# RWKV chunk step: the four small-matmul bursts of a chunk in one run, outputs in two alternating result banks

## The chip, the cores and the metric

The kernel runs on one core of a Trainium2 chip. The metric is device time in microseconds. The kernel before was timed in three runs: 2193.45, 2198.98 and 2200.49 us, median 2198.98. One more execution was profiled; it took 2194.43 us, of which 2192.7 us lie between the first and the last instruction (the span).

## The reference

One decoder layer over 2048 tokens of width 1024. After a norm, one wide projection feeds three branches: A, RWKV-7 time mixing with 8 heads of 64; B, sliding-window attention; C, attention over 256 memory tokens. Each branch is gated, projected back, and the three are summed by sigmoid gates, projected once more and added to x. The change is in branch A. Its heart is a recurrence over tokens, with a 64 x 64 state S for each head:

```python
def step(S, inp):
    r_t, w_t, k_t, v_t, a_t, b_t = inp
    sa = jnp.einsum('bhvk,bhk->bhv', S, a_t)
    S = S * w_t[:, :, None, :] + sa[..., None] * b_t[:, :, None, :] + v_t[..., None] * k_t[:, :, None, :]
    y = jnp.einsum('bhvk,bhk->bhv', S, r_t)
    return S, y
```

All is computed in float32. Large matmuls are done in three passes: each operand is split into a high and a low part of a shorter float32 format, and high x high, low x high and high x low are added up.

## The kernel before, in words

**Stages.** The 2048 tokens are worked in four superblocks of 512. In each, two streams of work are woven together: `stream_r` is branch A, `stream_f` is everything else that needs no result of A (memory attention, sliding-window attention, the merges of C and B, and eight gates). Then come the merge of A and the output phase (L1253 to L1268), and the next superblock. Nearly all of TensorE's instructions are dense matmuls of 128 x 128 x 512 in the helper `gemm3` (lines L471, L472, L473).

**Branch A.** `rwkv_prep` and `rwkv_inverse` turn each superblock into eight chunks of 64 tokens and park the per-chunk operands in DRAM. `rwkv_chain` (L863 on) then walks through the chunks one after another. The 8 heads lie as 4 pairs, a pair's two heads in the lower and upper 64 partitions. A chunk c needs from the chunk before it the state (in the tile Z), and does this:

- W (L928): 8 small matmuls from Q and Z into a bank of the tag `rw`. They use all 128 rows and half the columns of the array (128*64 in the profile; each matmul appears as two, so 16 in a burst).
- VectorE copies W to SBUF (L932).
- U (L943): 8 matmuls from B and W. They use a quarter of the array each (64*64).
- VectorE scales U into Z (L949, two instructions); S (L951), 4 matmuls of 128 x 128, makes the new state, and VectorE adds the decayed old one (L952, with SP from L941) into the next chunk's Z.
- The output of the chunk is a sum of two parts: `from_w` (L907), 8 matmuls from Q and Z in the form 128*64, and `from_u` (L902), 8 matmuls from B and U in the form 64*64. `from_w` comes first and starts the sum.

**Result bank.** The outputs of two chunks (`per` = 2) share one PSUM bank, `yps`. There is one such bank. When both chunks are in it, ScalarE copies it out (L912, in `take_y`), and only then may `from_w` of the next chunk start it anew. In an odd chunk the bursts come in the order W, `from_w` and then U, `from_u` of the chunk before. In an even chunk other than 0 (`later` in the code) it is W, `from_u` of the chunk before (which completes the bank), then U, and `from_w` behind it.

**What sets the order.** The engines' order is written out by a planner inside the kernel (`steps`, `lay_out`, `order`). It takes all instructions with their estimated durations and hand-over times, plays them through, and at each step gives an engine the ready instruction of lowest rank (a matmul of the array form now in use goes first). It then chains every engine's instructions in that order. A list of matmuls given to `together` becomes ready as one, and `behind` puts one instruction behind another; other matmuls may come between two such bursts.

**Pools.** PSUM has eight banks: two `mm` for dense results, two `rw`, two `as_` (attention, the transposes of the row scales and half of the output phase), one `oo` and one `yps`. `gp` is a pool of NG = 10 SBUF tiles of 2 KB per partition, named `g` in the profile, used by attention, gates, the parts of the merged result in the output phase and the rows of x loaded there (L1266) and added to the result (L1267). `dk` and `Pl` hold a superblock's per-chunk factors, two buffers each.

## Time and profile before

| | before |
|---|---|
| median of 3 runs | 2198.98 us (2193.45 to 2200.49) |
| profiled execution | 2194.43 us |
| its span | 2192.7 us |
| TensorE busy | 2168.5 us, 99% |
| VectorE, ScalarE busy | 1544.2 us, 818.7 us |
| chain bursts: L928, L907, L943, L902 | 512 matmuls each |
| bank copies L912 | 16 |

In a line of the timeline, the first number is the start in microseconds from the begin of the span, the second the length of the (merged) piece. Then come engine, line of the kernel, operation, the tile written and the tiles read, the form, and the number of instructions. A bracket at the end names idle time of the engine before it and what ended it. Matmuls overlap: the length of a dense one is longer than the distance to the next. PE is TensorE, DVE VectorE, ACT ScalarE, POOL GpSimd, SP the engine that issues most DMAs.

### The profile page before, as it was taken

How to read it: one execution, taken by the hardware profiler on the slowest of the kernel's cores; microseconds unless marked ns; L12 is line 12 of the kernel's file. 1: busy time of each engine (PE TensorE's matmuls, PEld its weight loads, DVE VectorE, ACT ScalarE, POOL GpSimd, SP SyncE). 2: the span in 40 equal slices, each digit the busy share in tenths (PEclk: the TensorE clock that was granted, in tenths of full speed). 3: DMA queues.
4: the chain of work that ended last, by engine and by line, in shares of the span. 5: the costliest groups of instructions: out<-in, count | busy, mean ns of one | idle time of the engine just before them, and what ended most of it. 6: DMA issues, size and time to landing. Idle time of an engine off the chain costs nothing.

```text
span 2192.7 us, 36285 instructions
## 1 busy us (share of the span) xinstructions
PE 2168.5 (99%) x13562; PEld 1793.1 (82%) x13562; DVE 1544.2 (70%) x3661; ACT 818.7 (37%) x1748; POOL 132.5 (6%) x166
## 2 busy tenths in 40 slices
PE   8999999999999999999999999999999999999999
PEld 7888788887888888888888888888878888887887
DVE  7789999567478889644537988954455798894332
ACT  5665554236344443203414434410423434430220
POOL 1001000001000000001000000000100010000100
PEclk9999999999999999999999999999999999999999
DMA  6978787978966566665776656675677666658456
GB/s 207 357 268 278 245 295 256 333 250 312 351 208 205 170 215 209 224 222 183 272 259 205 200 183 202 200 261 183 226 241 250 192 190 214 202 168 289 161 188 208
DMA packets 253151, 508.65 MB, mean 232 GB/s; under 512 B 38192, under 2 KB 119344, under 8 KB 252976
## 3 DMA queue, kind: packets, MB, share of 16 engines
q1 hardware_dynamic: 236848, 476.97, 65.4%
q10 hardware_dynamic: 16128, 29.37, 4.0%
q8 instruction: 107, 1.75, 0.3%
q14 instruction: 68, 0.56, 0.1%
HBM read 372.56 MB, written 133.69 MB: 231 GB/s over the span
## 4 chain that ended last, share of the span: by engine, by line
PE 90%; DMA 5%; DVE 3%; ACT 1%; issue 1%; POOL 0%; SPq 0%; ACTq 0%; DVEq 0%; POOLq 0%
PE mm L473 22%; PE mm L471 22%; PE mm L472 22%; PE oo L1212 1%; PE rw L951 1%; PE mm L1260 1%; PE mm L1261 1%; PE mm L1262 1%; PE rw L943 1%; PE rw L928 1%; PE yps L902 1%; PE yps L907 1%; PE rw L773 1%; PE rw L793 1%; DMA big<-fb 1%
## 5 line engine op out<-in xcount | busy, mean ns | idle before, releaser
L472 PE MATMUL mm<-hL,whl 128*128 128x512 f32 x1888 | 744.2, 394 | 0.0
L471 PE MATMUL mm<-hH,whl 128*128 128x512 f32 x1888 | 744.2, 394 | 0.0
L473 PE MATMUL mm<-hH,whl 128*128 128x512 f32 x1888 | 743.8, 394 | 0.0
L473 PEld LDWEIGHTS mm<-hH,whl 128*128 128x128 f32 x1888 | 354.8, 188 | 72.1 <-issue 1.2
L472 PEld LDWEIGHTS mm<-hL,whl 128*128 128x128 f32 x1888 | 354.8, 188 | 70.8 <-issue 0.7
L471 PEld LDWEIGHTS mm<-hH,whl 128*128 128x128 f32 x1888 | 354.8, 188 | 69.9 <-issue 0.3
L453 ACT ACTIVATE whl<-raw 128x512 fp32r<-128x512 f32 x178 | 111.3, 629 | 141.0 <-PE mm L473 93.8
L471 PE MATMUL mm<-yh,whl 128*128 128x512 f32 x384 | 151.3, 394 | 2.2 <-ACT gt L1228 1.5
L473 PE MATMUL mm<-yh,whl 128*128 128x512 f32 x384 | 151.7, 395 | 0.0
L472 PE MATMUL mm<-yl,whl 128*128 128x512 f32 x384 | 150.5, 392 | 0.0
L454 DVE TENSOR_TENSOR whl<-raw,whl 128x512 fp32r<-128x512 f32 x178 | 121.2, 685 | 36.9 <-ACT whl L453 35.7
L1228 ACT ACTIVATE gt<-mm 128x512 f32<-128x512 f32 x64 | 38.1, 595 | 209.0 <-PE mm L473 206.8
L830 DVE STREAM_SHUFFLE ibc<-Nc 128x496 f32<-128x496 f32 (+30 forms) x248 | 114.2, 472 | 0.1
L831 DVE TENSOR_TENSOR ibc<-ibc,Yi 128x496 f32<-128x496 f32 (+30 forms) x248 | 104.4, 421 | 3.7
L832 DVE TENSOR_TENSOR Yi<-Yi,ibc 128x496 f32<-128x496 f32 (+30 forms) x248 | 102.8, 414 | 0.7
L1267 DVE SCALAR_TENSOR_TENSOR g<-mm,g 128x512 f32<-128x512 f32 x16 | 11.1, 692 | 112.1 <-PE mm L1262 87.8
L471 PEld LDWEIGHTS mm<-yh,whl 128*128 128x128 f32 x384 | 72.1, 188 | 18.2 <-ACT gt L1228 1.7
L473 PEld LDWEIGHTS mm<-yh,whl 128*128 128x128 f32 x384 | 72.1, 188 | 14.7
L472 PEld LDWEIGHTS mm<-yl,whl 128*128 128x128 f32 x384 | 72.1, 188 | 14.6
L1243 DVE SCALAR_TENSOR_TENSOR gt<-gt,mm 128x512 f32<-128x512 f32 x32 | 22.0, 687 | 75.9 <-PE mm L473 75.6
L1185 ACT ACTIVATE g<-g,mxs,st 128x128 f32<-128x128 f32 x128 | 61.5, 484 | 25.9 <-DVE mxs L1178 25.9
L436 POOL TENSOR_SCALAR st<-st 128x4 f32<-128x4 f32 (+1 forms) x32 | 11.4, 355 | 938.9 <-DVE st L1027 434.6
(1801 smaller groups left out, 3600.4 us busy)
## 6 DMA issues: line engine op xcount, KB each, us to landing
whl<-k SPq DMA_DIRECT2D x486, 512.0 KB, 3.7
k<-whl SPq DMA_DIRECT2D x162, 512.0 KB, 4.8
raw<-in_w_in SPq DMA_DIRECT2D x118, 256.0 KB, 3.7
fq<-big SPq DMA_DIRECT2D x64, 256.0 KB, 4.6
fb<-big SPq DMA_DIRECT2D x64, 256.0 KB, 4.7
big<-fq SPq DMA_DIRECT2D x32, 512.0 KB, 6.2
big<-fb SPq DMA_DIRECT2D x32, 512.0 KB, 5.8
g<-in_x ACTq DMA_DIRECT2D x32, 256.0 KB, 5.2
```

The source lines that it names most:

```text
L453: S.activation(w[:, 0], raw, AF.Copy)
L454: V.tensor_tensor(w[:, 1], raw, w[:, 0].bitcast(F32), op=ALU.subtract)
L471: PE.matmul(out, lh, rh, start=i == 0, stop=False)
L472: PE.matmul(out, lh, rl, start=False, stop=False)
L473: PE.matmul(out, ll, rh, start=False, stop=i == n - 1)
L773: m = PE.matmul(g[:, c], BK[h, c0 + c], Q[h, c0 + c], start=True, stop=True)
L830: V.stream_shuffle(bc[:, :, :w], N_[:, :, s + 1:], [s] * 32)
L831: V.tensor_tensor(bc[:, :, :w], bc[:, :, :w], Y[:, :, s:s + 1].to_broadcast([128, n, w]), op=ALU.mult)
L832: V.tensor_tensor(Y[:, :, s + 1:], Y[:, :, s + 1:], bc[:, :, :w], op=ALU.add)
L1185: S.activation(P_, P_, AF.Exp, scale=r2[:, b, i:i + 1], bias=mx[:, b, i:i + 1], accum_out=mx[:, b, 2 + i:3 + i])
L1228: S.activation(t, gp, AF.Tanh, scale=0.5)
L1243: V.scalar_tensor_tensor(g, g, 1.0, pp, op0=ALU.add, op1=ALU.mult)
```

## The change

Within `rwkv_chain`, W, `from_w` of the same chunk and `from_u` of the chunk before become one burst, in that order, for every chunk. U is tied to the last matmul of that burst: a new table `follow` tells the planner that after this matmul TensorE takes nothing but U, and waits for it if need be. In chunk 0 there is no `from_u`, and no tie. Since `from_w` of a new pair now comes ahead of the `from_u` that completes the pair before, two result banks are in use by turns: `yps`, and one of the two `as_` banks. The pool of `g` tiles grows from 10 to 11, and `dk` and `Pl` go from two buffers to one.

```diff
-NG = 10
+NG = 11
...
-def steps(instructions, manual, groups, ahead=1000):
+def steps(instructions, manual, groups, follow, ahead=1000):
...
+    for a, b in follow.items():
+        byname[a].next = byname[b]
...
-    tile, wires, table = (128, 128), 0, 2
+    tile, wires, table, held = (128, 128), 0, 2, None
...
         for e, rs in ready.items():
+            if e == "PE" and held:
+                rs = {held: rs[held]} if held in rs else {}
             if rs:
...
-        can = [s for s, t in ready[e].items() if t <= at]
+        can = [s for s, t in ready[e].items() if t <= at and (e != "PE" or held in (None, s))]
...
-            tile = s.tile
+            tile, held = s.tile, s.next
...
+        ys = {}
+
         def yslot(i, c, e):
-            return yps[OD if (c + e) % 2 else EV, i, c % per // 2, e]
+            return ys[c // per][OD if (c + e) % 2 else EV, i, c % per // 2, e]
...
-            S.activation(full, yps.rearrange("p i t e v -> p (i t e v)"), AF.Copy)
+            S.activation(full, ys[last // per].rearrange("p i t e v -> p (i t e v)"), AF.Copy)
...
-            later = c % per == 0 and c
+            if c % per == 0:
+                ys[c // per] = (s_ps if c // per % 2 else y_ps)().rearrange("p (i t e v) -> p i t e v", i=n, t=per // 2, e=2)
             pw = rw_ps()[:, :n * C].rearrange("p (i t) -> p i t", i=n)
-            prev = burst([PE.matmul(pw[h, i], Q[:, i, e, :C], Z[:, i, e], start=True, stop=True) for i, e, h in HH], None, upds)
-            if later:
-                burst(from_u(c - 1), prev)
+            prev = burst([PE.matmul(pw[h, i], Q[:, i, e, :C], Z[:, i, e], start=True, stop=True) for i, e, h in HH] + from_w(c) + (from_u(c - 1) if c else []), None, upds)
             W = rp.tile([128, n, C], F32, name="W", bufs=1)
             V.tensor_copy(W, pw)
-            if later:
+            if c and c % per == 0:
                 take_y(c - 1)
-            if c % per == 0:
-                yps = y_ps().rearrange("p (i t e v) -> p i t e v", i=n, t=per // 2, e=2)
-            if not later:
-                burst(from_w(c), prev)
...
-            prev = burst([PE.matmul(pu[h, i], B[h, i, 0, :C], W[h, i], start=True, stop=True) for i, e, h in HH])
-            if later:
-                prev = burst(from_w(c), prev)
-            elif c:
-                prev = burst(from_u(c - 1), prev)
+            us = [PE.matmul(pu[h, i], B[h, i, 0, :C], W[h, i], start=True, stop=True) for i, e, h in HH]
+            if c:
+                follow[prev.ins.name] = us[0].ins.name
+            prev = burst(us, prev)
...
-            dk = xp.tile([128, 4, NC_], F32, name="dk", bufs=2)
-            Pl = xp.tile([128, 4, NC_], F32, name="Pl", bufs=2)
+            dk = xp.tile([128, 4, NC_], F32, name="dk", bufs=1)
+            Pl = xp.tile([128, 4, NC_], F32, name="Pl", bufs=1)
```

## The prediction

> **What bounds the kernel now.** I read the page first: busy time, clock, chain of waits.

> ```profile
> span 2192.7 us, 36285 instructions
> PE 2168.5 (99%) x13562; PEld 1793.1 (82%) x13562; DVE 1544.2 (70%) x3661; ACT 818.7 (37%) x1748; POOL 132.5 (6%) x166
> PE 90%; DMA 5%; DVE 3%; ACT 1%; issue 1%; POOL 0%; SPq 0%; ACTq 0%; DVEq 0%; POOLq 0%
> ```

> TensorE is idle for 2192.7 − 2168.5 = 24.2 us, and 90% of the chain that ended last lies on it. What sets the time is therefore how many nanoseconds pass from the start of one matmul to the start of the next. Busy time hides that, since overlapping matmuls count once; only the start column of the timeline shows it. Here is TensorE's timeline through two neighbouring chunks of the chain, c = 1 and c = 2 (start, length, line, tile, rows*columns of the array, count).

> ```profile
> 409.07 0.39 PE L473 MATMUL mm<-hH,whl 128*128 128x512 f32 x1
> 409.39 0.69 PE L928 MATMUL rw<-Zt,big 128*64 128x64 f32 x16
> 409.91 0.64 PE L907 MATMUL yps<-Zt,big 128*64 128x64 f32 x16
> 410.47 0.50 PE L471 MATMUL mm<-hH,whl 128*128 128x512 f32 x1
> 410.90 0.68 PE L943 MATMUL rw<-W,big 64*64 64x64 f32 x16
> 411.42 0.63 PE L902 MATMUL yps<-Zt,big 64*64 64x64 f32 x16
> 411.98 0.50 PE L472 MATMUL mm<-hL,whl 128*128 128x512 f32 x1
> 412.32 0.39 PE L473 MATMUL mm<-hH,whl 128*128 128x512 f32 x1
> ...
> 415.05 0.39 PE L472 MATMUL mm<-yl,whl 128*128 128x512 f32 x1
> 415.37 0.69 PE L928 MATMUL rw<-Zt,big 128*64 128x64 f32 x16
> 415.99 0.68 PE L902 MATMUL yps<-Zt,big 64*64 64x64 f32 x16
> 416.60 0.50 PE L473 MATMUL mm<-yh,whl 128*128 128x512 f32 x1
> 417.03 0.68 PE L943 MATMUL rw<-W,big 64*64 64x64 f32 x16
> 417.64 0.69 PE L907 MATMUL yps<-Zt,big 128*64 128x64 f32 x16
> 418.26 0.50 PE L471 MATMUL mm<-yh,whl 128*128 128x512 f32 x1
> 418.59 0.39 PE L472 MATMUL mm<-yl,whl 128*128 128x512 f32 x1
> 418.82 0.40 PE L473 MATMUL mm<-yh,whl 128*128 128x512 f32 x1
> ```

> L928 is W, L943 is U, L907 the output part from Z and Q (call it Yq), L902 the output part from U (Yu). Dense matmuls, L471 to L473, follow each other every 0.23 us (418.59 to 418.82). The step from a dense one into a burst takes 0.32 (409.07 to 409.39), the first dense one after a burst holds TensorE for 0.34 (411.98 to 412.32), and a single dense one between two bursts for 0.43 (410.47 to 410.90). A burst of 16 takes 0.52 when a burst of its own form follows (409.39 to 409.91), 0.56 to 0.62 when another form follows (409.91 to 410.47, 415.37 to 415.99).

> **The burst order, the main term.** The steady chunks have one dense matmul between the two visits (one of the 28 has two). Odd chunk: W, Yq | dense | U, Yu. Even chunk, where a result bank is finished and the next begun: W, Yu | dense | U, Yq. After the change both are W, Yq, Yu, U: two 128*64 bursts, then two 64*64 ones. No matmul is added or removed.

> Odd chunk. Before, from 409.07 to 412.32: 3.25 us with three dense matmuls in it. After: 0.32 + 0.52 + 0.56 + 0.52 + 0.56 + 0.34 = 2.82 with two of them; the displaced one runs elsewhere for 0.23, so 3.05. Saved: 0.20, which is 0.43 − 0.23: it is the lone dense matmul that is dear.

> Even chunk. Before, from 415.05 to 418.59: 3.54. After: the same 3.05. Saved: 0.49, since W, Yu and U, Yq each also changed form inside the visit.

> Chunks of these two kinds: c = 1, 3, 5, 7 and c = 2, 4, 6 in each of four superblocks, 16 and 12. Chunk 0 keeps its two visits, as it has no earlier Yu and its U is not tied; the last Yu runs alone as before. The last of the 28, an odd one, has W to U in the 1.51 us of the first (409.39 to 410.90):

> ```profile
> 2056.35 0.69 PE L928 MATMUL rw<-Zt,big 128*64 128x64 f32 x16
> ...
> 2057.86 0.68 PE L943 MATMUL rw<-W,big 64*64 64x64 f32 x16
> ```

> Sum: 16 × 0.20 + 12 × 0.49 = 9.1 us off TensorE. As dense work is waiting at every one of these places, I count all of it as time off the end. No DMA is added, and a chunk's fetch stands where it stood; its buffers come free with Yu, which in odd chunks is now ahead of U, so no later.

> **The wait that the lone dense matmul covered.** U reads W from SBUF, so VectorE must have copied it (L932). Nothing may run on TensorE between Yu and U now, so whatever the copy is late becomes idle TensorE, with all queued dense matmuls behind it. VectorE's copy, and what came before and after it, in three chunks:

> ```profile
> 410.12 0.42 DVE L932 COPY W<-rw 128x256 f32<-128x256 f32 x1 [0.46 <-PE rw L928]
> ...
> 954.55 0.43 DVE L949 TENSOR_TENSOR Zt<-rw,dk 64x256 f32<-64x256 f32 x1
> 955.03 0.71 PE L951 MATMUL rw<-Zt,big 128*128 128x128 f32 x4
> ...
> 471.26 0.69 PE L928 MATMUL rw<-Zt,big 128*64 128x64 f32 x16
> 471.58 0.69 DVE L454 TENSOR_TENSOR whl<-raw,whl 128x512 fp32r<-128x512 f32 x1 [1.14 <-ACT whl L453]
> ...
> 472.30 0.42 DVE L932 COPY W<-rw 128x256 f32<-128x256 f32 x1
> ```

> W starts at 409.39 and the copy ends at 410.54, 1.15 us later. The hand-over from VectorE to TensorE is not shown for an idle array and this pair; bounds are 0.05 (954.98 to 955.03, L949 to L951) and 0.36 (410.54 to 410.90, with a dense matmul in between). So U can start 1.20 to 1.51 after W. In the new order it stands 0.52 + 0.56 + 0.52 = 1.60 after W. The stall is nothing, with 0.09 to 0.40 in hand; what covers it is Yq and Yu. In the worst chunk of before, VectorE was at a weight split (L454, started at 471.58), and the copy ended at 472.72, 1.46 after W's start at 471.26: with the larger hand-over that is 1.82 and a stall of 0.22. At most that in all 28 chunks is 6.2 us, nothing is the other end; I take 0.3 us, since a copy behind a weight split is the exception. L949, which waits for U, comes about 0.1 us later in odd chunks, and dense matmuls fill that.

> **The second result bank.** It comes from the two banks that the attention uses. In the second superblock these are read last by L1203, and written next by the transposes for the following superblock:

> ```profile
> 892.15 0.67 DVE L1203 TENSOR_TENSOR g<-as__9632,over 128x512 f32<-128x512 f32 x1
> 1062.37 0.60 PE L539 MATMUL as__11147<-c_ident,rt 128*128 128x128 f32 x4
> ```

> The row of 954.55 shown above is from the fifth of that superblock's eight chunks, in the middle of this pause. I cost it at nothing; were an attention step in the way, it would cost that step's hold of a bank, about the 0.67 us eviction shown. ScalarE's copy of a finished bank now has two chunks before anybody needs that bank.

> **One more tile of the 2 KB pool; decay tiles single.** In the output phase the pool's ten tiles hold eight parts of the merged result, and two rows of x. With eleven, a third row can be loaded before its sum is due. That wait exists:

> ```profile
> 578.22 0.69 DVE L1267 SCALAR_TENSOR_TENSOR g<-mm,g 128x512 f32<-128x512 f32 x1 [3.62 <-DMA g<-in_x]
> ...
> 578.97 0.50 PE L1260 MATMUL mm<-whl,g 128*128 128x512 f32 x1 [0.85 <-DVE g L1267]
> PE mm L1260 <- DVE g L1267: 2.3, 3, 0.9
> ```

> TensorE stands for the bank that this sum empties, three times, 2.3 us in all. The gain is between 0 and 2.3; I take 2, as the wait is for exactly the load that comes earlier. Single decay tiles make the next superblock's first decays wait for the chain's last reads, which are done before the output phase begins: nothing.

> **The whole.** 9.1 + 2.0 − 0.3 = 10.8 us. The profiled execution took 2194.43, so 2183.6 by its scale. It stands 4.6 below the median of 2198.98 (runs from 2193.45 to 2200.49); I put the forecast halfway between 2183.6 and 2198.98 − 10.8 = 2188.2, at 2186.

> **The rivals.** *U waits for the copy in most chunks* (the other side). The planner orders VectorE by its own estimates, and may put a 0.69 us operation before the copy as in the chunk at 471.58, but started later: copy end at 1.15 + 0.69, plus 0.36, makes U ready at 2.20 and 0.60 late. Times 28 that is 16.8 us lost, against 10.8 + 0.3 gained: 5.7 slower, about 2202 halfway between the two scales. It decides from 0.4 us a chunk. For it: VectorE is 70% busy. Against: of the 25 chunks in which VectorE idled before the copy, it waited for W itself, 39.7 us in all:

> ```profile
> DVE W L932 <- PE rw L928: 39.7, 25, 4.6
> ```

> *The new order of everything else gives the gain back.* The planner lays all engines out anew, so the 24.2 us of idle TensorE will fall elsewhere. If it grows by a third, 8 us, 3 us remain: 2195. Nothing in the profile speaks for growth rather than loss; equally, a third less gives 2178.

> *The clock falls during the longer bursts.* [...] This trace halves the clock once, after TensorE had been busy for 3.61 of 8 us:

> ```profile
> 10.00:18.00 8.00, 3.61 (x24) 2.77 (x24) 7.79 (x21) 5.86 (x16) 2.52 (x6) 0.97 0.91 305
> 18.00:21.00 3.00, 2.88 (x14) 2.91 (x15) 3.00 (x7) 2.30 (x6) 0.30 (x1) 0.50 0.19 42
> ...
> 909.50:997.80 88.30, 87.27 (x842) 70.95 (x834) 37.41 (x87) 7.47 (x14) 0.61 (x1) 1.00 0.70 237
> ```

> Three microseconds at 0.50 lose 1.5; after each of 28 bursts that is 42 us, so 2186 + 42 = 2228. Against it stands the last row: a whole chain, with bursts that fill all of 409.39 to 411.98 but one dense matmul, at 1.00.

> **How the numbers follow.** Forecast 0.66, own range 2181 to 2191 (0 to 6.2 of stall, 0 to 2.3 of the pool's gain, and the two scales 4.6 apart). Gain given back 0.16, more gained through the new order 0.10, U late 0.07, clock 0.01. A measurement of this kernel can tell 0.3%, 6.6 us, from no change. Faster by that: the forecast but for 0.02, the 0.10, and a tenth of the given-back case, 0.75. Slower: U late in half its cases (its 5.7 is just under the bound), the clock, and 0.02 of given back, 0.07. Within: 0.18. The range goes from 2178, the lucky order, to 2195, the gain mostly given back.

> **What would show it.** Right: in the timeline each steady chunk is L928, the two output lines and the U line without a dense row between, U about 1.6 us after W, idle before it under 0.1; from the dense row before to the second dense row after, 2.8 us. The wait of L1260 for L1267 gone or smaller. TensorE's idle time still near 24 us and its matmul count unchanged. Wrong: an idle figure on U naming the W copy, 0.4 us or more; waits of attention tiles for the second bank; granted clock under 1.00 inside the chains; or idle time well above 24 us in places that the change doesn't touch.

## The result and the profile after

The changed kernel took 2188.3 us (median of 6 runs, 2184.27 to 2189.45) against 2199.08 for the kernel before (6 runs, 2193.45 to 2202.03): 0.995 of it, 95% interval 0.9935 to 0.9964, so 10.8 us faster. Timed again beside other kernels it took 2186.97, 0.9953 (0.9941 to 0.9965). The profiled execution took 2189.02 us.

The page, in the lines that answer to those of before:

```profile
span 2187.2 us, 36294 instructions
PE 2161.0 (99%) x13562; PEld 1793.7 (82%) x13562; DVE 1544.9 (71%) x3661; ACT 818.0 (37%) x1748; POOL 129.1 (6%) x166
PE 92%; DMA 4%; DVE 2%; ACT 1%; issue 1%; POOL 0%; SPq 0%; ACTq 0%; DVEq 0%; POOLq 0%
```

The matmul count is the same, and TensorE still sets the end. Its timeline through an odd chunk and the even one after it (lines have moved: W is now L935, Yq L913, Yu L908, U L944; dense matmuls L475 to L477):

```profile
926.93 0.39 PE L477 MATMUL mm<-hH,whl 128*128 128x512 f32 x1
927.25 0.69 PE L935 MATMUL rw<-Zt,big 128*64 128x64 f32 x16
927.76 0.64 PE L913 MATMUL yps<-Zt,big 128*64 128x64 f32 x16
928.33 0.68 PE L908 MATMUL yps<-Zt,big 64*64 64x64 f32 x16
928.85 0.63 PE L944 MATMUL rw<-W,big 64*64 64x64 f32 x16
929.41 0.50 PE L475 MATMUL mm<-hH,whl 128*128 128x512 f32 x1
929.74 0.40 PE L476 MATMUL mm<-hL,whl 128*128 128x512 f32 x1
...
932.96 0.40 PE L477 MATMUL mm<-yh,whl 128*128 128x512 f32 x1
933.29 0.69 PE L935 MATMUL rw<-Zt,big 128*64 128x64 f32 x16
933.80 0.64 PE L913 MATMUL as__9917<-Zt,big 128*64 128x64 f32 x16
934.37 0.51 PE L908 MATMUL yps<-Zt,big 64*64 64x64 f32 x10
934.66 0.27 PE L944 MATMUL rw<-W,big 64*64 64x64 f32 x2
...
934.83 0.22 PE L908 MATMUL yps<-Zt,big 64*64 64x64 f32 x1
934.83 0.51 PE L944 MATMUL rw<-W,big 64*64 64x64 f32 x11
935.27 0.50 PE L475 MATMUL mm<-yh,whl 128*128 128x512 f32 x1
935.61 0.39 PE L476 MATMUL mm<-yl,whl 128*128 128x512 f32 x1
```

The four bursts are one run. The odd chunk takes 2.81 us from the dense matmul before to the second one after. The even chunk takes 2.65, and there rows of U stand between rows of Yu: U began 0.29 us after Yu, not 0.52.

I call a visit the time from the dense matmul before W to the second one after U, less 0.227 us for each dense matmul in it (the median step from one dense matmul to the next in both traces). Means over all chunks of the two traces: even 2.87 before, 2.23 after; odd 2.57 before, 2.36 after. That is 12 × 0.63 + 16 × 0.21 = 10.9 us.

Where TensorE waits in the changed kernel (who, for whom, us in all, times, longest), and the granted clock in five stretches (TensorE's busy time comes first after the comma, the clock third from the end):

```profile
PE rw L944 <- DMA big<-fb: 6.7, 3, 3.0
...
PE as__16590 L1260 <- DVE g L1267: 0.8, 1, 0.8
...
PE as__21565 L1260 <- DVE g L1267: 0.3, 1, 0.3
```

```profile
914.30:917.70 3.40, 3.40 (x17) 2.82 (x16) 0.11 (x1) 0.60 (x1) 0.00 (x0) 1.00 0.95 327
917.80:921.10 3.30, 0.36 (x2) 0.00 (x0) 1.17 (x2) 0.00 (x0) 0.00 (x0) 1.00 0.94 356
922.55:925.96 3.41, 3.41 (x13) 3.06 (x13) 0.72 (x3) 0.00 (x0) 0.00 (x0) 0.50 1.03 419
1980.69:1984.10 3.41, 1.00 (x18) 0.93 (x19) 0.90 (x2) 0.00 (x0) 0.00 (x0) 1.00 0.99 384
1984.10:1987.50 3.40, 3.40 (x14) 3.02 (x13) 0.56 (x2) 0.00 (x0) 0.00 (x0) 0.50 1.03 414
```

The wait for the output bank fell from 2.3 to 1.1 us. But U of chunk 0 waits 6.7 us for its operand B, and twice the clock is halved behind it for 3.4 us, which by an estimate (half of 3.4) costs 1.7 each. In the profiled execution of before this wait was three times 1 us, with no half clock behind it:

```profile
PE rw L943 <- DMA big<-fb: 3.0, 3, 1.0
```

So between the two profiled executions: −10.9 for the bursts, −1.2 for the bank, +3.7 for chunk 0, +3.4 for the clock, −5.0 in all, against 2194.43 − 2189.02 = 5.4 measured. The medians differ by 10.8; the profiled execution of before stands 4.6 below its median, that of the changed kernel 0.7 above. The record has the granted clock of every timed run: the 47 runs of before in the comparisons below average 0.9975, and only three of them have the 0.999 of the profiled one; the changed kernel's runs average 0.9973 and, timed again, 0.9977. So most executions of before ran at half clock for longer than the profiled one did (by an estimate from these figures, 0.0015 of 2199 us, some 3 us lost), and the +3.4 belongs to the pair of executions that was profiled. It is not shown to be a cost of the change.

### The profile page after: what moved, and what is told of

Its sections match the earlier page's. It is cut to its first block, busy times and chain, and to the rows that moved or that the text cites. A ratio compares the mean times of both kernels' runs of the same rounds, so it can differ in the third digit from the quotient of the medians.

```text
span 2187.2 us, 36294 instructions
## 1 busy us (share of the span) xinstructions
PE 2161.0 (99%) x13562; PEld 1793.7 (82%) x13562; DVE 1544.9 (71%) x3661; ACT 818.0 (37%) x1748; POOL 129.1 (6%) x166
## 4 chain that ended last, share of the span: by engine, by line
PE 92%; DMA 4%; DVE 2%; ACT 1%; issue 1%; POOL 0%; SPq 0%; ACTq 0%; DVEq 0%; POOLq 0%
PE mm L475 23%; PE mm L477 23%; PE mm L476 22%; PE rw L951 1%; PE oo L1212 1%; PE mm L1260 1%; PE mm L1262 1%; PE mm L1261 1%; PE rw L935 1%; DMA big<-fb 1%; PE rw L777 1%; PE rw L944 1%; PE rw L797 1%; DMA fb<-big 1%; DMA out<-g 1%
## 5 line engine op out<-in xcount | busy, mean ns | idle before, releaser
L477 PE MATMUL mm<-hH,whl 128*128 128x512 f32 x1888 | 745.4, 395 | 0.0
L475 PE MATMUL mm<-hH,whl 128*128 128x512 f32 x1888 | 745.4, 395 | 0.0
L477 PEld LDWEIGHTS mm<-hH,whl 128*128 128x128 f32 x1888 | 355.1, 188 | 72.7 <-issue 1.2
L475 PEld LDWEIGHTS mm<-hH,whl 128*128 128x128 f32 x1888 | 355.2, 188 | 69.7 <-issue 0.3
L475 PE MATMUL mm<-yh,whl 128*128 128x512 f32 x384 | 150.7, 392 | 1.6 <-ACT gt L1228 1.5
L477 PE MATMUL mm<-yh,whl 128*128 128x512 f32 x384 | 151.5, 395 | 0.0
L475 PEld LDWEIGHTS mm<-yh,whl 128*128 128x128 f32 x384 | 72.1, 188 | 17.0 <-ACT gt L1228 1.7
L477 PEld LDWEIGHTS mm<-yh,whl 128*128 128x128 f32 x384 | 72.1, 188 | 14.5
L1267 DVE SCALAR_TENSOR_TENSOR g<-mm,g 128x512 f32<-128x512 f32 x16 | 11.1, 691 | 83.5 <-PE mm L1262 83.5
```

What stands on the lines that cost most here:

```text
L475: PE.matmul(out, lh, rh, start=i == 0, stop=False)
L477: PE.matmul(out, ll, rh, start=False, stop=i == n - 1)
```

## The experiments

Four things were to be settled: the size of the two kinds of chunk, the pool's part, whether the W copy needs its cover, and what chunk 0's wait costs. Each kernel was timed beside the kernel before, whose median was 2198.4 to 2199.0 in these comparisons.

### The pool back at ten

```diff
-NG = 11
+NG = 10
```

> The changed kernel with the pool of g tiles back at ten; burst order, two result banks and single decay tiles stay. If the eleventh tile gives what the prediction gave it, this kernel is 2 us slower than the changed one, 8.8 faster than before (0.996 of it). Rival, the tile gives nothing: it stands with the changed kernel at 10.8 below before (0.995), and the idle time of L1260 on its bank is the same in both.

Measured: 2193.55 us, 0.997 of before (0.9955 to 0.9984). By the medians the tile gave some 5 us, not 2, though this interval and the changed kernel's (0.9935 to 0.9964) overlap. The profile says the same: TensorE idles 4.5 us before L1260, against 1.1 in the changed kernel, the longest time 2.7, and the clock is halved behind that one (over the whole profiled execution it averages 0.996, against 0.997).

### The pool alone

```diff
-NG = 10
+NG = 11
...
-            dk = xp.tile([128, 4, NC_], F32, name="dk", bufs=2)
-            Pl = xp.tile([128, 4, NC_], F32, name="Pl", bufs=2)
+            dk = xp.tile([128, 4, NC_], F32, name="dk", bufs=1)
+            Pl = xp.tile([128, 4, NC_], F32, name="Pl", bufs=1)
```

> The kernel before with eleven g tiles and single decay tiles, and its old order of bursts. Prediction's term: 2 us faster than before (0.999), the idle time before L1260 falls from 2.3 us. Rival, the new plan alone gives more: over 5 us faster. If the single decay tiles hold up the next superblock it is slower than before.

Measured: 2195.86 us, 0.9987 (0.9976 to 0.9998): 2.9 faster, near the predicted term, and single decay tiles hold nothing up. Its profile, with the old order of bursts, has 4.7 us of wait of U of chunk 0, the longest 2.0, and a half-clock stretch behind it (the mean clock of this execution is 0.997, that of the profiled one of before 0.999). So that wait can be longer than in the profile of before, with half clock behind it, without the new order too.

### Only the even chunks in one run

```diff
-... + from_w(c) + (from_u(c - 1) if c else []), None, upds)
+... + from_w(c) + (from_u(c - 1) if c and c % per == 0 else []), None, upds)
...
-            prev = burst(us, prev)
+            prev = burst(us, prev if c % per == 0 else None)
+            if c % per:
+                prev = burst(from_u(c - 1), prev)
```

(and no tie of U in odd chunks)

> The changed kernel, but only the even chunks 2, 4 and 6 run their four bursts in one; odd chunks have the old order W, Yq, one dense matmul, U, Yu. By the sum of the prediction: 12 x 0.49 = 5.9 us of the 9.1 stay, with the pool's part 7.9 below before, 3 slower than the changed kernel. If in addition U overlaps Yu in even chunks, as the starts in the changed kernel's trace suggest (U 0.29 to 0.35 us after Yu's start there, 0.52 in odd chunks), 12 x 0.2 = 2.4 more are saved there, about 10 below before and within 1 us of the changed kernel. Rival, all chunks save alike: 12/28 of the gain, some 5 below before.

Measured: 2186.8 us, 0.9947 (0.9929 to 0.9965), level with the changed kernel. That rules out that all chunks save alike (5 below before), and fits the overlap, but the interval is 8 us wide, so it does not size the odd chunks. Before sizes could be told apart, the wait of chunk 0 had to go.

### U of chunk 0 later

```diff
+LATE = 5000
...
-        ready[s.eng][s] = max([at] + [seen_by(s, b) for b in s.before])
+        ready[s.eng][s] = max([at] + [seen_by(s, b) for b in s.before]) + s.late
...
             if c:
                 follow[prev.ins.name] = us[0].ins.name
+            else:
+                late.extend(m.ins.name for m in us)
```

(`late` is a list of instructions whose `late` the planner sets to LATE ns.)

> The changed kernel, with U of chunk 0 put 5 us later in the planner's reckoning, so that 68 dense matmuls stand between W and U of chunk 0 in place of 46 (84 in place of 62 in the first superblock). Theory: the waits of U of chunk 0 for its fetch (3.1, 1.1 and 2.7 us in the changed kernel's profile) and the two stretches of 3.4 us at half clock behind the longer ones (1.7 us each) are pure loss; without them 5 to 9 us faster than the changed kernel, 15 to 20 below before, clock 0.999. Rival, the wait only moves on to chunk 1 or its fetch, or the clock falls for another reason: no gain, clock 0.997 as before.

Measured: 2178.84 us (2176.16 to 2181.19), 0.9909 of before (0.9891 to 0.9926): 9.5 us faster than the changed kernel (8.1 against its later timing), where 5 to 9 were expected. The wait of U is gone from the list, and past the first 22 us the clock stays at 1.00 to the end (0.999 over the whole execution). In 100 us of the second superblock, the chain among them, the profile shows no idle TensorE:

```profile
900.00:1000.00 100.00, 100.00 (x1020) 82.92 (x1019) 43.90 (x101) 14.07 (x28) 2.44 (x3) 1.00 0.69 234
```

This version beats both kernels.

### The same wait made longer

```diff
-LATE = 5000
+LATE = -3000
```

> The changed kernel with U of chunk 0 put earlier in the planner's reckoning: 33 dense matmuls between W and U of chunk 0 in place of 46 (49 for 62 in the first superblock). Theory: U then waits 13 x 0.23 = 3.0 us longer for the same fetch in three superblocks, 4 to 6 us each, and the clock is halved behind each of these waits (1.7 us each, two to three times): 9 us of wait and 0 to 3 of clock more than the changed kernel, 2197 to 2201, clock 0.997 or less. Rival, the wait is made up later in the chain: within 2 us of the changed kernel.

Measured: 2209.56 us, 1.0047 of before (1.0032 to 1.0062): slower than before, by more than expected. The profile has the reason (first the wait, then the clock around the longest one):

```profile
PE rw L948 <- DMA big<-fb: 18.8, 4, 5.6
```

```profile
924.00:927.40 3.40, 0.00 (x0) 0.00 (x0) 0.00 (x0) 0.00 (x0) 0.00 (x0) 1.00 0.90 324
927.40:934.20 6.80, 6.03 (x29) 4.97 (x30) 1.08 (x3) 0.00 (x0) 0.00 (x0) 0.50 0.88 351
```

Against the changed kernel timed beside it (the next one) the wait is 13.4 us longer (18.8 less 5.4). Past the start-up the trace counts 30.7 us at half clock against 6.8: 23.9 more, by the same estimate worth at most 11.9, and less where U is still waiting in it. Together that is up to 25.3; the two profiled executions differ by 24.1, the medians by 22.6. I had reckoned with single half-clock stretches; behind three of the four waits it was a double one, as in the 6.80 us above.

### The changed kernel again

> The changed kernel once more beside the others, for its place on the same chip: 2188, 0.995 of before, with waits of U of chunk 0 of 1 to 3 us and the clock at 0.997 to 0.998.

Measured: 2186.97 us, 0.9953 (0.9941 to 0.9965), with 5.4 us of wait, one half-clock stretch in the chains, and a mean clock of 0.997 in the profiled execution.

### The old order with U of chunk 0 later

The edit is the same `late` list, in the kernel before.

> The kernel before (old order of bursts, one result bank, ten g tiles), with U of chunk 0 put 5 us later in the planner's reckoning. Theory: what it gains against the kernel before is the wait of U of chunk 0 and the clock behind it, 3 to 8 us; and from here to the kernel with late U0 and the new order (2178.8) is what the order and the pool give without that wait: 28 visits measured in the traces save 12 x 0.63 + 16 x 0.21 = 10.9 us, the pool 1 to 2, so it should stand at 2191, 0.9965 of before. Rival, moving U of chunk 0 helped only through the new order: no change against before.

Measured: 2194.71 us, 0.9977 (0.9965 to 0.999): 4.3 faster than before, as expected for the wait, but 3.7 above the 2191 named. The wait of U is gone; the new plan waits elsewhere:

```profile
PE mm L1267 <- DVE g L1274: 3.1, 2, 2.1
...
PE as__6372 L1267 <- DVE g L1274: 2.1, 1, 2.1
```

This is the output phase's wait for a row of x, 5.2 us here, with 6.8 us at half clock behind it. The plan of the kernel before had 2.3 us of it, with the same ten tiles.

### Only even chunks in one run, U of chunk 0 later

The edits of the two kernels above together.

> Late U0, and only the even chunks in one run; odd chunks in the old order. By the visits in the traces the odd chunks save 16 x 0.21 = 3.3 us, so this is 3.3 slower than the kernel with late U0, 2182. Rival, from the even_only run, which was no slower than the changed kernel: odd chunks save nothing, 2179.

Measured: 2182.94 us, 0.9925 (0.9911 to 0.9939): 4.1 slower than with all chunks in one run. The two intervals overlap, and this kernel's profile has 2.1 us of wait for a row of x where the other has 0.3, so the medians alone do not size the odd chunks. The traces do: the odd visits take 2.60 us on average here and 2.39 with all chunks in one run, 3.4 us in sum. So the odd chunks do give their 3 us, against the rival read from the earlier run.

### The pool back at ten, U of chunk 0 later

> Late U0, new order, the pool of g tiles back at ten. The pool's part without the scatter of chunk 0's wait. By the two runs on the pool so far (5.2 between the changed kernel and the one with ten tiles, 2.9 between the kernel before and the one with eleven) 3 to 5 us slower than with eleven, 2182 to 2184, with idle time of L1260 on its bank of 2 us or more and the clock halved behind the longer of these waits. Rival, the prediction's size: 1 to 2 us and no half clock.

Measured: 2182.95 us, 0.9928 (0.9915 to 0.9941): 4.1 slower than with eleven (here too the intervals overlap; the traces decide). The waits, 4.7 us against 0.3 with eleven tiles, and the clock behind them:

```profile
PE as__6372 L1266 <- DVE g L1273: 3.0, 1, 3.0
...
PE mm L1266 <- DVE g L1273: 1.7, 2, 1.0
```

```profile
577.70:581.10 3.40, 1.35 (x6) 1.15 (x7) 0.69 (x1) 0.36 (x1) 0.00 (x0) 1.00 0.50 196
581.20:584.60 3.40, 3.40 (x9) 2.65 (x8) 1.38 (x2) 0.81 (x2) 0.00 (x0) 0.50 0.72 214
```

With ten tiles and the old order 2194.71 were measured, with ten and the new order 2182.95: 11.8 less with the wait of chunk 0 out of the way. Not all of that is the order and the second bank: the plan with the old order waits 0.5 us more for the rows of x, and is at half clock for 3.4 us more behind it, worth 1.7 by the same estimate, in the two profiles.

### Half the cover taken away

Yu moves from ahead of U to behind it, and `take_y` with it; U follows Yq.

```diff
-... + from_w(c) + (from_u(c - 1) if c else []), None, upds)
+... + from_w(c), None, upds)
...
             prev = burst(us, prev)
+            if c:
+                prev = burst(from_u(c - 1), prev)
```

> Late U0, and Yu moved from ahead of U to behind it: W, Yq, U, Yu, still without a dense matmul between. It takes half of the cover of the W copy away. U would then stand 1.08 us after W, but the copy ends 1.15 after W and the hand-over takes 0.06 to 0.22, as the changed kernel's trace shows. Theory: U idles 0.13 to 0.29 us in each of 28 chunks, 4 to 8 us, and the overlap of U with Yu in even chunks may go, up to 2 us more: 2183 to 2189. Rival, the cover is not needed: 2179 to 2181.

Measured: 2189.56 us, 0.9953 (0.994 to 0.9965): 10.7 slower than with the cover, just beyond the expected range. One chunk of it (W L939, Yq L917, U L946, Yu L912; VectorE's copy L941 and SP L944):

```profile
931.81 0.42 DVE L944 TENSOR_TENSOR SP<-Zt,Pl 64x256 f32<-64x256 f32 x1
932.42 0.69 PE L939 MATMUL rw<-Zt,big 128*64 128x64 f32 x16
932.94 0.64 PE L917 MATMUL yps<-Zt,big 128*64 128x64 f32 x16
933.09 0.42 DVE L944 TENSOR_TENSOR SP<-Zt,Pl 64x256 f32<-64x256 f32 x1
933.54 0.42 DVE L941 COPY W<-rw 128x256 f32<-128x256 f32 x1
934.02 0.68 PE L946 MATMUL rw<-W,big 64*64 64x64 f32 x16 [0.44 <-DVE W L941]
```

Here the planner has put half of SP ahead of the copy, the copy ends 1.54 us after W, and U stands idle for it. It is so in seven chunks; in five others an operation of 0.69 us is ahead of the copy. It is the rival "U waits for the copy" made real. In the two profiles the 28 visits take 8.1 us more than with the cover, 4.6 of it in ten waits of U for the copy; a half-clock stretch at 271.8 us, worth 1.7 by the same estimate, that the kernel with the cover does not have is not the cover's (mean clock 0.998, against 0.999). So a shorter cover and a later copy take most of the order's gain.

### Halves of the result bank exchanged

```diff
-            return ys[c // per][OD if (c + e) % 2 else EV, i, c % per // 2, e]
+            return ys[c // per][EV if (c + e) % 2 else OD, i, c % per // 2, e]
```

(and EV and OD exchanged where the output is unpacked)

> Late U0, and the halves of the result bank exchanged: the output of head e of chunk c goes to the upper 64 partitions where (c + e) is even, and the later unpacking is exchanged with it. Theory: U overlaps the end of Yu where the two use different quarters of the array. Then the overlap moves from even chunks (12) to odd chunks (16): U starts 0.29 us after Yu in odd chunks and 0.52 in even ones, odd visits shrink by 0.17 us and even ones grow by 0.17, 0.7 us faster in sum, which the timing can't tell. Rival, the overlap belongs to the change of result bank or to the copy's timing in even chunks: it stays in even chunks.

Measured: 2179.22 us, 0.9908 (0.9888 to 0.9928), as with U of chunk 0 later alone (two runs). Its timeline through an odd and an even chunk (Yu is L912, U L948):

```profile
943.16 0.51 PE L912 MATMUL as__9917<-Zt,big 64*64 64x64 f32 x10
943.45 0.27 PE L948 MATMUL rw<-W,big 64*64 64x64 f32 x2
...
949.03 0.68 PE L912 MATMUL as__9917<-Zt,big 64*64 64x64 f32 x16
949.55 0.63 PE L948 MATMUL rw<-W,big 64*64 64x64 f32 x16
```

The overlap has moved: the undisturbed visits are now 2.19 in odd chunks (ten of the 16) and 2.36 in even ones. It goes by the halves of the partitions, of which a matmul of the form 64*64 here reads one and writes one. U reads and writes the head's own half. Yu reads that half too; where it also writes it, U began 0.52 us after Yu (949.03 to 949.55), and where it writes the other half, 0.29 (943.16 to 943.45).

### U untied

```diff
-            if c:
-                follow[prev.ins.name] = us[0].ins.name
```

(U of chunk 0 stays late)

> Late U0, new order, but U no longer tied to the last Yu: the planner is free to put dense matmuls between. It does so in a few of the 28 chunks only, since it prefers a matmul of the array form in use. Theory: each such place costs 0.2 us, under 2 us in sum, within 2178 to 2182. Rival, the tie does the work: the gain of the order, 10 us, is gone.

Measured: 2181.23 us, 0.992 (0.9905 to 0.9934), 2.4 slower than tied, which is inside the intervals. In seven chunks a dense matmul now stands between Yu and U. Such a visit takes 2.71 to 2.73 us, 0.36 more than an undisturbed odd one and 0.52 more than an even one, where the overlap goes as well; I had named 0.2. Over all 28 visits the two profiles differ by 2.6 us. The tie is worth 2 to 3 us; the order does the work.

## Why the prediction was right, and where it was not

*The forecast.* 2186 predicted, 2188.3 and 2187.0 measured; 10.8 us saved predicted and measured. The sum's agreement to the tenth is partly luck: two terms were too small, the bursts by 1.8 and the pool by 1 to 3, so something took 3 to 5 us back. In the profiled executions that was the wait of chunk 0, which the sum left out, with the clock behind it; how much of it stands between the medians is not shown. The 2186 itself leaned half on the scale of the profiled execution, at clock 0.999 an uncommonly fast one; by the median's scale the same sum gives 2188.2.

*The burst order, main term.* Right in kind and place. The odd chunks' 0.20 is 0.21 in the trace. The even chunks' 0.49 is 0.63: the step that failed took U for a burst behind Yu, 0.52 after it, where the trace has it begin 0.29 after Yu, among Yu's rows. 9.1 predicted, 10.9 in the traces, and in the timing with ten tiles 11.8, of which some 2 belong to the output phase. The text says that one of the 28 visits had two dense matmuls between; two had, which changes nothing in the sum.

*The wait for the W copy.* Taken at 0.3 us. In the changed kernel's trace the visits where U is held up are those of chunk 4 in three superblocks and chunk 2 in the first (2.31 in place of 2.19 us), 0.5 in all. The price of losing the cover, 16.8 us with a copy queued behind 0.69 us of other work in every chunk, was not tested as it stands; half the cover away, with half of SP or 0.69 us of other work in front in twelve chunks, cost 8.1 in the visits and 10.7 at the medians.

*The second bank.* Costed at nothing; no wait on it appears.

*The pool.* 2 predicted; 2.9, 4.1 and 5.2 in three comparisons, each uncertain by a few us. The term took the 2.3 us of wait in one plan for the most that the tile can give; three other plans with ten tiles have 4.5, 4.7 and 5.2 us there. And it took only TensorE's own idle time: in those three plans the clock was halved behind the wait as well (for 6.8 us with the old order, 3.4 with the new one and chunk 0's wait gone).

*The clock.* The rival had the wrong cause. With chunk 0's wait gone, the chains with all their long bursts ran at 1.00 throughout (0.999 over the whole execution); in the changed kernel 0.50 stood behind waits of 3.0 and 2.6 us. That a run of small matmuls lowers the clock was an assumption; no run shows it, nor the 42 us reckoned from it. One row of the profile of before pointed to idle time instead (3.61 us busy of 8, then 0.50), and I did not ask what a wait would cost in clock. "Once" leaves out a second stretch there, in the last 0.8 us of the span.

*The signs.* The visits came as named, 2.81 us in odd chunks and U 1.60 after W, and shorter in even ones, 2.65 and 1.38. TensorE idles 26.2 us in place of 24.2. One sign of being wrong did appear, a granted clock under 1.00 inside two chains; its cause was chunk 0's wait and not the bursts. In the rival that gives the gain back, 8 us on 2186 make 2194, not 2195.

*What the prediction passed over.* "Chunk 0 keeps its two visits" was right, and its wait of 3.0 us for B stood in the waits of before, but I treated it as a constant. It lies on the path, it varies, and behind two of its three occurrences in the changed kernel (3.0 and 2.6 us) the clock was at 0.50 for 3.4 us; moving U of chunk 0 back by 22 dense matmuls was worth 9.5 us with the new order, nearly as much as the change, and 4.3 with the old one, where new waits in the output phase took part of it back. What varies is the transfer. In the second to fourth superblock of both kernels U starts 0.13 to 0.15 us after the fetch of B has landed, and the fetch is issued 3.4 to 3.9 us before TensorE is free for U. But it took 4.45, 4.61 and 4.81 us to land before, and 6.34, 4.70 and 6.08 in the changed kernel. Why it lands later, and whether the new order makes the wait longer, stays open: four profiles with the new order, whole or in the even chunks, have 5.4 to 6.7 us of this wait, two with the old one 3.0 and 4.7; 46 dense matmuls (62 in the first superblock) stand between W and U of chunk 0 in both.

## What to carry to other kernels

Where one engine is 99% busy, count the distance from start to start, not busy time: a lone dense matmul between two bursts of small tiles cost 0.43 us instead of 0.23. Before taking away such a filler, check what it covered, from the producer's start to the end of the copy, and keep the difference positive. And look at the longer waits of the busy engine, even if the change does not touch them: here one transfer's landing time, at three places with 0.87 to 1.05 us of wait each before the change, was worth 9.5 us after it, against 10.8 for the whole change.

## What the runs showed of the hardware that was not expected

*U's matmuls started before Yu's last.* In program order all of Yu precedes U. In the even chunk of the changed kernel's trace shown above, U's first matmul starts at 934.66 and Yu's last at 934.83; in the odd chunk U starts at 928.85, 0.52 us after Yu's first and behind all of Yu. With the output halves exchanged it is the other way round: 0.29 us from Yu's start to U's in the odd chunk (943.16 to 943.45), 0.52 in the even one (949.03 to 949.55).
